# Third leaf and sums of the last gate/up pair on VectorE, another step order, and other first buffers for the down projection

## The chip, the cores and the metric

The kernel runs on one core of a Trainium2 chip. A core has a matrix engine (TensorE, "PE" in the profile, with its weight loads apart as "PEld"), an elementwise engine (VectorE, "DVE"), an engine for functions and copies (ScalarE, "ACT"), a general engine (GpSimd, "POOL"), and one that issues transfers (SyncE, "SP"). Matrix products land in eight PSUM banks and are read from there by VectorE or ScalarE. GpSimd's transfers can add what they bring to what lies at the target ("accumulating"). The metric is the device time of the whole program in microseconds, the median of three runs.

## What is computed

A block of a hybrid network on 1024 positions with a width of 1024: an mLSTM mixer and a sparse attention, their outputs merged, then a gated feed-forward part of width 2816. The change touches only the feed-forward part:

```python
h = h + mixed @ w_out[l]
f = rms_norm(h, g_norm_ffn[l])
h = h + (jax.nn.silu(f @ w_gate[l]) * (f @ w_up[l])) @ w_down[l]
...
return rms_norm(h, g_final)
```

## The kernel before

Everything is float32. A product is made of three matmuls (`chain3`): both operands are split into a high and a low part; high times high, high times low and low times high are added in PSUM. ScalarE copies the high part, VectorE subtracts it for the low part (`operand`, `op`).

**Gate and up.** The 2816 columns of w_gate and w_up are worked in 11 pairs of 128 columns, `s` = 0 to 10, each for gate (`G`, `w` = 0) and up (`U`, `w` = 1). A pair's product with the normed rows is done by a scheme with seven products in place of eight, numbered `q`; three of them (2, 4 and 3, the "leaves") are done by the same scheme once more, across gate and up. `whole` (L2578) does a product of the first level: q 6, 7, 1 and 5, in the step texts `g6`, `u7` and so on. `two` (L2616) does the leaves 2 and 4 (`d` for the pair before, `D` for the same pair), `third` (L2635) leaf 3 (`t` and `T`). `begin` loads the raw weights' first halves, `rest` the second ones. The raw weights lie in four buffers of 512 KB; `RB[s, w, 0]` holds the first half of the rows, `RB[s, w, 1]` the second; `RH` is the right part of the first.

The sums of raw weights are made in place. Some are made by VectorE (`combine`), others by accumulating transfers of GpSimd that fetch the addend from HBM again (`gather`). Behind product 7, leaf 3 needs the first half's left part to which the second half is added: two such transfers for each of gate and up. A third kind adds one result to another inside SBUF (`moved`). Gated results go to HBM, to `d_gu`, two rows for each pair.

**The order.** A step text (L2696) is gone through for the pairs 2 to 10; it gives each step a rank. A planner (`Plan`) then places the steps: each engine has a clock, each step a cost written out by hand and the steps that it depends on, and the step that can start first, or with the lower rank among those, is next on its engine. The engines then run their queues strictly in that order. `V5`, `V2` and `V1` are the costs of VectorE's operations; `lat` is the time to a transfer's landing that the planner assumes.

**The down projection** adds over 22 rows of `d_gu` in two groups of pairs (five and six), again with seven products in place of eight, `q` in the order 1, 5, 6, 3, 7, 2, 4 in the first group. `RSL` and `SLOTS` say which buffer takes which operand: numbers below 16 are `sl`, 16 to 27 `q`, 28 to 30 `ra`, from 36 on `lateU`. The late buffers lie where the low parts of the normed rows (`UTL`) lie, so they are free when the last product of gate and up has read those. The results of the first group are copied from PSUM into `acc`, and an accumulating transfer adds `d_h`, the sum so far, to each.

Of the kernel before, what the change touches and what calls it, by code (L numbers as in the profile page):

```python
# [8 lines left out]
F32 = mybir.dt.float32  # L9
F32R = mybir.dt.float32r  # L10
AF = mybir.ActivationFunctionType
ALU = mybir.AluOpType
# [171 lines left out]
def body(ctx, tc, a, out, stop=None, dbg=None):  # L184
# [46 lines left out]
    class Stream:  # L231
# [13 lines left out]
        def dma(self, upto):  # L245
            while self.nd <= min(upto, len(self.jobs) - 1):
                src, (n, m), *_ = self.jobs[self.nd]
                t = self.pool.tile([P, T], F32, name=f"raw{self.nd}", tag="raw", bufs=self.bufs)
                v = t[:, 0:n * m].rearrange("p (n m) -> p n m", n=n)
                col = 0  # L250
                for s in (src if isinstance(src, list) else [src]):
                    w = s.shape[-1]
                    nc.sync.dma_start(v[:, :, col:col + w], s)
                    col += w
                self.raw[self.nd] = v
                self.nd += 1
# [104 lines left out]
    with ExitStack() as sa:  # L361
# [60 lines left out]
        V = (("DVE", 700.0),)  # L422
# [1700 lines left out]
    def slot_ap(n, dt):  # L2123
        if n > 35:
            if not late:
                late.append(utp.tile([P, 8, 2, 512], F32R, name="lateU", tag="UTL", bufs=1))
            return cast32(late[0][:, n - 36]) if dt == F32 else late[0][:, n - 36]
        if n < 16:
            if n not in held or held[n].dtype != dt:
                held[n] = q2p.tile([P, 2, 512], dt, name=f"sl{n}_{len(held)}", tag=f"sl{n}", bufs=1)  # L2130
            return held[n]
        if n < 28:
            z = (n - 16) % 2
            return q1_tile((n - 16) // 2, dt)[:, 2 * z:2 * z + 2, :]
        if n < 31:
            return RAW[n - 28]
        return (WHI, WLO)[(n - 31) // 2][(n - 31) % 2]
# [194 lines left out]
    def rows4(b):  # L2332
        return b.ap.rearrange("p a (k c) -> p (a k) c", k=2)
# [18 lines left out]
    def col(s, w, z, h):  # L2352
        return lambda: rows4(RB[s, w, z])[:, :, h]
# [17 lines left out]
    def moved(b, x):  # L2371
        pl.step((("Pool", 850.0),), lambda e: nc.gpsimd.dma_start(b.ap, x.ap, accum_op=ALU.add), [x], [b], lat=5000.0)
# [7 lines left out]
    def combine(dst, x, y, alu, reads, writes):  # L2380
        ew(V5, dst, x, y, alu, reads, writes)
# [179 lines left out]
    def begin(s):  # L2561
        p = ST[s] = Pair()
        p.A, p.C = ([pl.buf(), pl.buf()] for _ in range(2))
        p.x, p.b = {2: pl.buf(), 4: pl.buf(), 3: pl.buf()}, {2: pl.buf(), 4: pl.buf(), 3: pl.buf()}
        p.out, p.own = {}, {}
        for w in range(2):
            load_raw(s, w, 0, w)
        for w in range(2):
            gather(RH[s, w], raw_src(s, w, 1, HI), col(s, w, 0, HI))
# [8 lines left out]
    def whole(s, q, w):  # L2578
        p, r0, rh, r1 = ST[s], RB[s, w, 0], RH[s, w], RB.get((s, w, 1))
        left = col(s, w, 0, LO)  # L2580
        if q == 6:
            combine(left, left, col(s, w, 0, HI), ALU.add, [rh], [r0])
        elif q == 7:
            combine(left, left, col(s, w, 1, HI), ALU.subtract, [r1], [r0])
            if w == U:
                gather(r1, raw_src(s, U, 1, k=1), row(s, U, 1, 0))
        level1(s, w, q)
        if q == 7:
            gather(r0, raw_src(s, w, 1, HI), left)
            gather(r0, raw_src(s, w, 1, LO), left)  # L2590
        acc_ = p.C if q == 5 else p.A
        product(s, w, q, acc_[w], q in (1, 5), q in (7, 5))
        t = p.out[q, w] = copied(acc_[w], place_of(s, q, w))
        if q == 5:
            moved(p.out[6, w], t)
            ew(V5, lambda: t.ap, lambda: t.ap, lambda: p.out[7, w].ap, ALU.add, [p.out[7, w]], [t])
            if w == 1:
                gated(s, 1, 1, p.out[5, G], p.out[5, U])
# [35 lines left out]

    def third(s, n):  # L2635
        p = ST[s]
        g, u = RB[s, G, 0], RB[s, U, 0]
        quarter = lambda r, k: (lambda: rows4(r)[:, 2 * k:2 * k + 2, LO])
        wa, wb, wc, wd = quarter(g, 0), quarter(u, 0), quarter(g, 1), quarter(u, 1)
        if n in PACKS:  # L2640
            b = slot_buf(RING4[nop[0] % 4], F32R)
            nop[0] += 1
            if n == 6:
                ew(V1, wb, wb, wd, ALU.add, [], [u])
                ew(V1, wa, wb, wa, ALU.subtract, [u], [g])
            elif n == 7:
                ew(V1, wc, wc, wa, ALU.subtract, [], [g])
                ew(V1, wa, wd, wa, ALU.subtract, [u], [g])
            for m, k in enumerate(PACKS[n]):
                form = lambda hl, m=m: b.ap[:, hl, 256 * m:256 * m + 256].rearrange("p (k c) -> p k c", k=2)  # L2650
                x, r = {1: (wa, g), 2: (wc, g), 6: (wa, g), 5: (wb, u), 7: (wa, g), 3: (wc, g), 4: (wd, u)}[k]
                act(400.0, lambda form=form: form(0), x, AF.Copy, [r], [b])
                ew(V1, lambda form=form: form(1), x, lambda form=form: cast32(form(0)), ALU.subtract, [r, b], [b])
                p.own[3, k] = b, m
        chains(s, p, 3, n)
        gathers(p, 3, n, p.out[6, G], p.out[6, U])
        if n == 4:
            gated(s, 0, 1, p.out[6, G], p.out[6, U])

    def run(s, text):  # L2660
        for t in text.split():
            kind, what = t[0], t[1:]
            if kind in "gu":
                whole(s, int(what), "gu".index(kind))
            elif kind == "d" and s - 1 >= 2:
                two(s - 1, int(what))
            elif kind == "D":
                two(s, int(what))
            elif kind == "t" and s - 1 >= 2:
                third(s - 1, int(what))  # L2670
            elif kind == "T":
                third(s, int(what))
            elif t == "begin" and s + 1 < NS:
                begin(s + 1)
            elif t == "rest":
                rest(s)

    flat(0)
    lates = []
    pl.boost = -60  # L2680
# [12 lines left out]
    last()  # L2693
    pl.boost = 0
    for s in range(2, NS):
        run(s, "g1 d3 u1 d4 rest g6 u6 t1 t2 g7 t6 t5 t7 t3 u7 t4 begin g5 D2 u5 D1 D6 D5 D7")  # L2696
    run(NS - 1, "D3 T1 T6 T2 T5 T7 D4 T3 T4")

# [2 lines left out]
    HEAD7, HEAD4, SUMMED = 3, 1, (0,)  # L2703
    OPS = (20, 21, 22, 23, 10, 13, 12, 15, 31, 33, 32, 34)
    OPL = list(OPS + (6, 7, 9, 3, 4, 8))
    RSL = (0, 24, 26, 28, 11, 1, 25, 27, 29, 14, 16, 18, 30, 36, 38, 17, 19, 2, 37, 5, 40, 41, 42, 43)
    LATE = 80
    V, SUM = V5, V5
    allf = list(fsb.values())
    gLb = slot_buf(39)  # L2710

    def load2(n, src, reads=()):

        bs = pieces(n)
        dma(lambda: slot_ap(n, F32), lambda: src.rearrange("p (a c) -> p a c", a=2), reads, bs, kb=512)
        return bs

    def op(src, n=None):
# [293 lines left out]
```

## Time and profile before

| | |
|---|---|
| median of three timed runs | 1534.38 us (1533.55 to 1534.68) |
| the profiled execution | 1532.0 us |
| its span | 1530.2 us |
| TensorE busy | 1509.6 us, 99% of the span |
| VectorE, ScalarE, GpSimd busy | 77%, 57%, 18% |
| HBM read and written | 169.95 and 62.48 MB |

A page gives each engine's busy time, groups of instructions by line, and the chain of waits that ended last. Rows of the timeline have a start and a duration in us, the engine, the line, what is written and read by the program's names, and in brackets the idle time of the engine before it and what ended it. A table of stretches has for each the busy time of PE, PEld, DVE, ACT and POOL with the number of instructions, then TensorE's granted clock, the DMA engines' busy share and GB/s. A busy TensorE may still run at half the clock; the column says so.

### The profile page before, as it was taken

To read this page: it belongs to the slowest core of one execution; us is meant where nothing else is said; L and a number is where in the kernel's file an instruction comes from. 1 tells how busy PE (TensorE), PEld (TensorE's weight loads), DVE (VectorE), ACT (ScalarE), POOL (GpSimd) and SP (SyncE) were. 2 spreads that over 40 slices of the span, in tenths; PEclk is the share of its full clock that TensorE was granted. 3 is DMA by queue.
4 is the path that set the end of the run, shared out by engine and by line. 5 is a ranking of instruction groups with operands and counts; after the bars stand their busy time and mean duration, and the time that the engine had idled before them with its cause. 6 is when DMAs were issued, how large, how long until landed. Compare 5 with 4: busy or idle time off the path is not lost.

```text
span 1530.2 us, 23966 instructions
## 1 busy us (share of the span) xinstructions
PE 1509.6 (99%) x8274; PEld 1304.4 (85%) x8274; DVE 1181.0 (77%) x2540; ACT 874.8 (57%) x1940; POOL 282.1 (18%) x399
## 2 busy tenths in 40 slices
PE   9999999999999999999999999999999998999997
PEld 8978888888988888888888888888888887888886
DVE  7877878456988798956665596778777776898996
ACT  8535444576988798865453464445445544465443
POOL 7500003333100111011020012222222222110000
PEclk9999999999999999999999999999999999999999
DMA  7458657859232622128466245477777779857002
GB/s 250 155 137 247 203 184 242 245 201 260 70 90 66 162 70 87 43 62 301 133 210 189 83 125 125 75 145 145 152 145 151 153 145 253 263 124 234 1 1 111
DMA packets 201924, 230.93 MB, mean 151 GB/s; under 512 B 11978, under 2 KB 156487, under 8 KB 201546
## 3 DMA queue, kind: packets, MB, share of 16 engines
q1 hardware_dynamic: 152090, 188.22, 38.2%
q0 software_dynamic: 49424, 40.85, 17.2%
q8 instruction: 65, 1.06, 0.3%
q14 instruction: 57, 0.47, 0.1%
q10 hardware_dynamic: 288, 0.33, 0.1%
HBM read 169.95 MB, written 62.48 MB: 152 GB/s over the span
## 4 chain that ended last, share of the span: by engine, by line
PE 93%; DMA 3%; DVE 2%; ACT 1%; issue 0%; SPq 0%; POOL 0%; DVEq 0%; POOLq 0%; ACTq 0%
PE PS L2330 38%; PE PSA L309 6%; PE PSA L311 6%; PE PSA L310 6%; PE T L1634 4%; PE d L309 3%; PE d L310 3%; PE d L311 3%; PE obank L1665 2%; PE obank L1667 2%; PE PS L309 2%; PE PS L311 2%; PE br L310 2%; PE br L309 2%; PE PS L310 2%; PE br L311 2%
## 5 line engine op out<-in xcount | busy, mean ns | idle before, releaser
L2091 DVE TENSOR_TENSOR sl<-PS,sl 128x256 f32<-128x256 f32 (+1 forms) x202 | 100.5, 510 | 71.6 <-PE PS L2330 58.8
L2330 PE MATMUL PS<-sl,sl 128*128 128x512 f32 (+1 forms) x513 | 118.5, 385 | 0.0
L2330 PEld LDWEIGHTS PS<-sl,sl 128*128 128x128 f32 x513 | 95.3, 188 | 19.4 <-DVE acc L2091 0.2
L2094 ACT ACTIVATE sl<-PS 128x512 f32<-128x512 f32 x90 | 53.7, 598 | 94.2 <-PE PS L2330 73.6
L1654 DVE TENSOR_TENSOR TL<-T,TH 128x512 fp32r<-128x512 f32 (+1 forms) x151 | 90.6, 617 | 19.4 <-ACT TH L1645 17.8
L2330 PE MATMUL PS<-q,wh 128*128 128x512 f32 x420 | 101.2, 391 | 0.0
L2330 PE MATMUL PS<-UTH,wl 128*128 128x256 f32 (+1 forms) x392 | 97.7, 323 | 1.2 <-ACT wl L2094 1.0
L2330 PEld LDWEIGHTS PS<-q,wh 128*128 128x128 f32 x420 | 77.3, 188 | 15.0
L1645 ACT ACTIVATE TH<-T 128x512 fp32r<-128x512 f32 (+1 forms) x151 | 79.3, 539 | 18.6 <-PE T L1634 16.8
L2330 PE MATMUL PS<-q,wl 128*128 128x512 f32 x348 | 84.2, 391 | 0.0
L2330 PE MATMUL PS<-UTH,wh 128*128 128x256 f32 (+1 forms) x344 | 82.4, 315 | 0.0
L1665 PE MATMUL obank<-TH,VHL 128*128 128x256 f32 x263 | 75.6, 310 | 0.0
L2330 PEld LDWEIGHTS PS<-UTH,wl 128*128 128x128 f32 x392 | 68.8, 193 | 7.6 <-ACT wl L2094 1.2
L2330 PEld LDWEIGHTS PS<-q,wl 128*128 128x128 f32 x348 | 63.8, 188 | 12.3
L2091 DVE TENSOR_TENSOR sl<-sl,sl 128x512 f32<-128x512 f32 (+2 forms) x87 | 57.2, 662 | 21.9 <-DMA d_h<-sl 10.1
L309 PE MATMUL d<-UTH,whi 128*128 128x512 f32 x176 | 71.4, 406 | 0.1
L311 PE MATMUL d<-UTH,wlo 128*128 128x512 f32 x176 | 69.1, 393 | 0.0
L310 PE MATMUL d<-UTL,whi 128*128 128x512 f32 x176 | 69.0, 392 | 0.0
L1667 PE MATMUL obank<-TL,VHL 128*128 128x256 f32 x264 | 68.2, 282 | 0.0
L2094 ACT ACTIVATE sl<-sl 128x512 f32<-128x512 f32 (+1 forms) x73 | 44.4, 625 | 40.4 <-DVE sl L2091 26.6
L309 PE MATMUL PSA<-UTH,wOwhi 128*128 128x512 f32 (+1 forms) x172 | 67.1, 390 | 0.0
L311 PE MATMUL PSA<-UTH,wOwlo 128*128 128x512 f32 (+1 forms) x180 | 66.9, 372 | 0.0
(1392 smaller groups left out, 4654.4 us busy)
## 6 DMA issues: line engine op xcount, KB each, us to landing
d_gu<-sl SPq DMA_DIRECT2D x44, 256.0 KB, 2.8
rA<-in_w_in SPq DMA_DIRECT2D x18, 512.0 KB, 4.9
q<-d_mg SPq DMA_DIRECT2D x32, 256.0 KB, 3.4
ra<-in_w_gate SPq DMA_DIRECT2D x16, 512.0 KB, 5.7
d_rep<-d_row SPq DMA_DIRECT2D x8, 960.0 KB, 6.9
sl<-in_w_up POOLq DMA_DIRECT2D x29, 256.0 KB, 5.3
ra<-in_w_up SPq DMA_DIRECT2D x12, 512.0 KB
raw<-in_w_in SPq DMA_DIRECT2D x10, 512.0 KB, 4.7
```

The source lines that it names most:

```text
L309: nc.tensor.matmul(ps, ah, bh, start=first, stop=False)
L310: nc.tensor.matmul(ps, ah, bl, start=False, stop=False)
L311: nc.tensor.matmul(ps, al, bh, start=False, stop=last)
L1634: nc.tensor.transpose(pt[:, z, P * r:P * r + P], e, ident)
L1645: nc.scalar.activation(hl[0][:, 0:m], pt[:, 0:m], AF.Copy)
L1654: nc.vector.tensor_tensor(hl[1][:, 0:m], pt[:, 0:m], cast32(hl[0])[:, 0:m], ALU.subtract)
L1665: nc.tensor.matmul(po, vv, th[:, z, :], start=(st[1] == 0), stop=False)
L1667: nc.tensor.matmul(po, vv, tl[:, z, :], start=False, stop=(st[1] == st[2]))
L2091: return pl.step(alts, lambda e: ENG[e].tensor_tensor(out_(), x(), y(), alu), reads, writes, **kw)
L2094: return pl.step((("ACT", cost),), lambda e: nc.scalar.activation(out_(), x(), fn, scale=scale), reads, writes, **kw)
L2330: nc.tensor.matmul(ps, x, y, start=first and n == 0, stop=last and n == 2, skip_group_check=True)
```

## The change

The last pair (s = 10) is treated apart. In `whole`, ahead of the difference for product 7, VectorE writes the left part plus the second half's left part into a buffer of its own, `p.last[w]`, from which `third` then takes leaf 3's weights; the four transfers that made the same sum in place are gone for this pair. Up's sum of two row blocks, for which a transfer fetched one again, is made by VectorE from what lies there. The two results that `moved` added are added by VectorE. Ahead of the last pair the planner's costs of VectorE's operations are set to 625, 350 and 350 (`quick`). The last pair has a step text of its own, in which leaf 3 of pair 9 comes early, and its own leaves behind. In the down projection the operands of the first group take other buffers (`RSL`), VectorE's cost is 690 again, and the planner assumes that a load lands after 5000 and not 2000 as long as the results of no product have been copied.

```diff
@@ -2581,18 +2581,27 @@
         elif q == 7:
+            if s == NS - 1:
+                d = p.last[w] = piece(w)
+                combine(lambda: four(d.ap), left, col(s, w, 1, LO), ALU.add, [r0, r1], [d])
             combine(left, left, col(s, w, 1, HI), ALU.subtract, [r1], [r0])
-            if w == U:
+            if w == U and s == NS - 1:
+                combine(row(s, U, 1, 0), row(s, U, 1, 0), row(s, U, 1, 1), ALU.add, [], [r1])
+            elif w == U:
                 gather(r1, raw_src(s, U, 1, k=1), row(s, U, 1, 0))
         level1(s, w, q)
-        if q == 7:
+        if q == 7 and s < NS - 1:
             gather(r0, raw_src(s, w, 1, HI), left)
             gather(r0, raw_src(s, w, 1, LO), left)
...
         if q == 5:
-            moved(p.out[6, w], t)
+            if s < NS - 1:
+                moved(p.out[6, w], t)
+            else:
+                v = p.out[6, w]
+                ew(V5, lambda: v.ap, lambda: v.ap, lambda: t.ap, ALU.add, [t], [v])
@@ -2634,8 +2643,11 @@
-        g, u = RB[s, G, 0], RB[s, U, 0]
-        quarter = lambda r, k: (lambda: rows4(r)[:, 2 * k:2 * k + 2, LO])
+        g, u = (p.last.get(w, RB[s, w, 0]) for w in (G, U))
+        if p.last:
+            quarter = lambda r, k: (lambda: four(r.ap)[:, 2 * k:2 * k + 2])
+        else:
+            quarter = lambda r, k: (lambda: rows4(r)[:, 2 * k:2 * k + 2, LO])
@@ -2675,6 +2687,10 @@
+    def quick():
+        nonlocal V5, V2, V1
+        V5, V2, V1 = (("DVE", 625.0),), (("DVE", 350.0),), (("DVE", 350.0),)
@@ -2693,8 +2709,10 @@
     for s in range(2, NS):
-        run(s, "g1 d3 u1 d4 rest g6 u6 t1 t2 g7 t6 t5 t7 t3 u7 t4 begin g5 D2 u5 D1 D6 D5 D7")
-    run(NS - 1, "D3 T1 T6 T2 T5 T7 D4 T3 T4")
+        if s == NS - 1:
+            quick()
+        run(s, "t1 g1 u1 t6 t2 t5 t7 d3 d4 g6 t3 t4 u6 rest g7 g5 u7 D1 D6 D2 u5 D5 D7 D3 T1 T6 T2 T5 D4 T7 T3 T4" if s == NS - 1 else "g1 d3 u1 d4 rest g6 u6 t1 t2 g7 t6 t5 t7 t3 u7 t4 begin g5 D2 u5 D1 D6 D5 D7")
+    run(NS - 1, " ")
@@ -2703,16 +2721,16 @@
-    RSL = (0, 24, 26, 28, 11, 1, 25, 27, 29, 14, 16, 18, 30, 36, 38, 17, 19, 2, 37, 5, 40, 41, 42, 43)
+    RSL = (24, 26, 30, 28, 11, 25, 27, 16, 29, 14, 17, 18, 0, 36, 38, 1, 19, 2, 37, 5, 40, 41, 42, 43)
-    V, SUM = V5, V5
+    V = SUM = V5 = (("DVE", 690.0),)
...
-        dma(lambda: slot_ap(n, F32), lambda: src.rearrange("p (a c) -> p a c", a=2), reads, bs, kb=512)
+        dma(lambda: slot_ap(n, F32), lambda: src.rearrange("p (a c) -> p a c", a=2), reads, bs, kb=512, lat=5000.0 if not acct else 2000.0)
```

Three places in the engines' queues. First GpSimd, from the end of pair 9 to the start of the copies into `acc`. Before (the rows of w_gate and w_up, and the two from `sl` to `sl` behind them, belong to the last pair; those of w_down to the down projection's first sums):

```order
L2369 DMA ra_8650<-in_w_gate 128x4x128
L2369 DMA ra_8649<-in_w_up 128x2x256
L2734 DMA q_4_6_12593<-in_w_down 128x512
L2369 DMA sl_1_8686<-in_w_up 128x4x128
L2369 DMA ra_8650<-in_w_gate 128x4x128
L2734 DMA q_5_6_12606<-in_w_down 128x512
L2734 DMA sl_16_9345<-in_w_down 128x512
L2369 DMA sl_1_8686<-in_w_up 128x4x128
L2372 DMA sl_16_9354<-sl_16_9435 128x512 x2
L2734 DMA sl_16_12841<-in_w_down 128x512
L2734 DMA ra_8649<-in_w_down 128x512
```

The same place of the changed kernel:

```order
L2752 DMA q_4_6_12654<-in_w_down 128x512
L2752 DMA q_5_6_12672<-in_w_down 128x512
L2752 DMA q_0_6_12798<-in_w_down 128x512
L2752 DMA sl_16_12831<-in_w_down 128x512
L2752 DMA ra_8649<-in_w_down 128x512
```

The seven transfers of the last pair are gone; the five sums of w_down are there in both.

Second TensorE, at the end of gate and up. The rows of `UTH` and `UTL` are the last pair's last product, those with two `sl`, or with `wl` and `wh`, or `q`, are products of the down projection. Before:

```order
L2330 MATMUL PS_8646<-UTH,wh_8652 128x256
L2330 MATMUL PS_8646<-UTL,wh_8652 128x256
L2330 MATMUL PS_8646<-UTH,wh_8652 128x256 x2
L2330 MATMUL PS_8646<-UTL,wh_8652 128x256
L2330 MATMUL PS_8646<-UTH,wh_8652 128x256
L2330 MATMUL PS_8642<-sl_16_9650,sl_16_9475 128x512 x3
L2330 MATMUL PS_8641<-sl_16_9650,sl_16_9475 128x512 x3
L2330 MATMUL PS_8645<-sl_16_9650,sl_16_9475 128x512 x3
L2330 MATMUL PS_8643<-sl_16_9650,sl_16_9475 128x512 x3
L2330 MATMUL PS_8642<-sl_16_9748,sl_16_9594 128x512 x3
```

The changed kernel:

```order
L2330 MATMUL PS_8647<-sl_16_9748,sl_16_9594 128x512 x3
L2330 MATMUL PS_8642<-sl_16_9748,sl_16_9594 128x512 x3
L2330 MATMUL PS_8641<-sl_16_9748,sl_16_9594 128x512 x3
L2330 MATMUL PS_8640<-sl_16_9748,sl_16_9594 128x512 x3
L2330 MATMUL PS_8646<-UTH,wh_8652 128x256
L2330 MATMUL PS_8646<-UTL,wh_8652 128x256
L2330 MATMUL PS_8646<-UTH,wh_8652 128x256 x2
L2330 MATMUL PS_8646<-UTL,wh_8652 128x256
L2330 MATMUL PS_8646<-UTH,wh_8652 128x256
L2330 MATMUL PS_8647<-wl_8653,wh_8651 128x512 x3
```

The products with `sl_16_9650` and `sl_16_9748`, twelve matmuls each, stood behind the last product and now stand ahead of it. The product of the third pair in the third step (q = 6) reads buffers of the same names again, `sl_16_9748` and `sl_16_9594`; from the last product of gate and up to there stand 40 rows of three matmuls before, and 32 in the changed kernel.

Third SP, the loads into the late buffers and the load behind them. Before:

```order
L2105 DMA lateU<-d_gu_132 128x1024
L2105 DMA lateU<-in_w_down 128x1024
L2105 DMA lateU<-d_gu_134 128x1024
L2105 DMA lateU<-d_gu_136 128x1024
L2105 DMA lateU<-d_gu_138 128x1024
L2105 DMA lateU<-d_gu_140 128x1024
L2105 DMA d_gu_145<-sl_16_9354 128x512
L2105 DMA lateU<-d_gu_142 128x1024
L2105 DMA lateU<-in_g_final 128x1024
L2105 DMA sl_16_9354<-in_w_down 128x1024
```

The changed kernel:

```order
L2105 DMA lateU<-d_gu_132 128x1024
L2105 DMA lateU<-in_w_down 128x1024
L2105 DMA lateU<-d_gu_134 128x1024
L2105 DMA d_gu_145<-sl_16_9354 128x512
L2105 DMA lateU<-d_gu_136 128x1024
L2105 DMA lateU<-d_gu_138 128x1024
L2105 DMA lateU<-d_gu_140 128x1024
L2105 DMA lateU<-d_gu_142 128x1024
L2105 DMA lateU<-in_g_final 128x1024
L2105 DMA sl_16_9354<-in_w_down 128x1024
```

The write of a gated result from `sl_16_9354`, for which the load into the same buffer waits, moved from the seventh to the fourth place.

More of the change, by code (lines that the diff above doesn't have):

```diff
@@ L2564, in begin @@
         p.x, p.b = {2: pl.buf(), 4: pl.buf(), 3: pl.buf()}, {2: pl.buf(), 4: pl.buf(), 3: pl.buf()}
-        p.out, p.own = {}, {}
+        p.out, p.own, p.last = {}, {}, {}
         for w in range(2):
```

## The prediction

> **What bounds the kernel now.** First the head of the page, then the table of stretches, which says where TensorE (PE) is not busy.
>
> ```profile
> span 1530.2 us, 23966 instructions
> PE 1509.6 (99%) x8274; PEld 1304.4 (85%) x8274; DVE 1181.0 (77%) x2540; ACT 874.8 (57%) x1940; POOL 282.1 (18%) x399
> 900.00:1250.00 350.00, 350.00 (x1970) 307.19 (x1969) 269.74 (x502) 170.96 (x311) 93.63 (x78) 1.00 0.68 138
> 1250.00:1312.00 62.00, 53.70 (x308) 47.46 (x308) 43.98 (x89) 28.19 (x55) 12.78 (x13) 0.94 0.85 220
> 1312.00:1520.00 208.00, 208.00 (x945) 173.22 (x944) 184.97 (x320) 106.29 (x200) 14.08 (x16) 1.00 0.39 118
> ```
>
> TensorE sets the end nearly everywhere. From 900 us on it is idle in one place only, 1250 to 1312 us, for 62.00 − 53.70 = 8.3 us, and there its granted clock is 0.94 and not 1.00. That place is the last gate/up pair with the first loads of the down projection. The changed kernel issues the same matmuls, so only this loss can be won, and only new idle time can be lost. TensorE's rows in the order of time give its pieces (in brackets the idle time before each):
>
> ```profile
> 1255.15 1.70 PE L2330 MATMUL PS<-sl,wl 128*128 128x256 f32 x12 [1.10 <-DVE sl L2091]
> 1282.96 0.39 PE L2330 MATMUL PS<-UTH,wl 128*128 128x256 f32 x1 [1.03 <-ACT wl L2094]
> 1283.68 0.51 PE L2330 MATMUL PS<-UTH,wl 128*128 128x256 f32 x2 [0.22 <-DVE wl L2091]
> 1291.00 0.95 PE L2330 MATMUL PS<-sl,wh 128*128 128x256 f32 x6 [0.90 <-DVE sl L2091]
> 1296.08 0.74 PE L2330 MATMUL PS<-sl,wh 128*128 128x256 f32 x4 [3.05 <-DVE wh L2091]
> 1298.83 1.65 PE L2330 MATMUL PS<-sl,wh 128*128 128x256 f32 x6 [2.00 <-DVE sl L2091]
> ```
>
> The sum is 8.30 us. VectorE and ScalarE are named, but they waited themselves; their own rows, and the chain of waits, say for what:
>
> ```profile
> 1253.95 0.69 DVE L2091 TENSOR_TENSOR sl<-sl,sl 128x512 f32<-128x512 f32 x1 [2.08 <-DMA sl<-sl]
> 1281.76 0.63 ACT L2094 ACTIVATE q<-sl 128x512 fp32r<-128x512 f32 x1 [3.56 <-DMA sl<-in_w_down]
> 1295.00 0.43 DVE L2091 TENSOR_TENSOR sl<-sl 128x256 f32<-128x256 f32 x1 [2.59 <-DMA sl<-in_w_up]
> 1297.62 0.69 DVE L2091 TENSOR_TENSOR sl<-sl,sl 128x512 f32<-128x512 f32 x1 [1.59 <-DMA sl<-sl]
> ...
> 1275.63 10.29 DMA sl<-in_w_up
> 1287.77 9.83 DMA sl<-sl
> 1298.83 46.21 PE PS L2330 x226
> ```
>
> Accumulating transfers of GpSimd, 10.29 and 9.83 us long, carry the chain to TensorE's row at 1298.83; the 3.05 us hang on another of them, for which VectorE waits at 1295.00. The 1.03 at 1282.96 is ScalarE's queue: a down-projection copy of w_down stands ahead of a gate/up copy and waits for its load. The idle time has a second price, seen when the stretch is cut into pieces of 6.8 us:
>
> ```profile
> 1284.40:1291.20 6.80, 5.90 (x39) 5.23 (x38) 6.10 (x11) 4.41 (x9) 2.21 (x2) 1.00 1.14 198
> 1291.20:1298.10 6.90, 2.57 (x18) 2.09 (x17) 2.52 (x6) 2.18 (x5) 0.86 (x1) 1.00 1.09 296
> 1298.10:1304.90 6.80, 6.07 (x26) 5.98 (x27) 5.13 (x11) 2.39 (x5) 0.00 (x0) 0.50 0.72 258
> 1516.60:1523.40 6.80, 4.60 (x36) 4.28 (x35) 4.84 (x21) 2.70 (x8) 0.00 (x0) 1.00 0.21 78
> 1523.40:1530.20 6.80, 0.00 (x0) 0.00 (x0) 1.71 (x5) 1.09 (x2) 0.00 (x0) 0.50 0.42 157
> ```
>
> A piece with 4.3 idle us is followed by one at clock 0.50; so is, at the program's end, a piece with 2.2 idle us. A piece with 0.9 is not. The half clock made 6.07 busy us do the work of 3.04. So the loss to be won is 8.30 + 3.04 = 11.3 us.
>
> **The change part by part.** *Removed:* seven GpSimd transfers of the last pair, two into each first half of gate and up, one into up's second half, two of one result into another. They hold both ends of the chain above. *Added:* five VectorE operations of 128x512 with both operands in SBUF: two sums kept for the third leaf, one sum of up's rows, two sums of results. The 1297.62 row has the price of one, 0.69 us: 3.45 us in all. VectorE is busy 43.98 of the 62.00 us, so 18 us of idle time cover them; without cover each would cost TensorE up to 0.69.
>
> *Moved:* the third leaf of pair 9 stands earlier. The last pair's second-half loads (two of 512 KB on SP) are issued in the other order; their consumers stand behind other operations that TensorE still has work ahead of. I cost this at nothing, with bounds 0 and 2 us. *The planner's cost for loads* (5000 for 2000) puts ScalarE's copies of w_down behind the gate/up copies, so the 1.03 and the 0.22 go too. SP's writes of gated results and GpSimd's sums of w_down (five, as before) remain; with seven transfers fewer beside them they land no later.
>
> *What is late next* inside the pair: where a PSUM bank must be emptied by VectorE directly ahead of the next product, TensorE waits for part of an operation of 0.42 to 0.69. The new order has two tight places of this kind, near 1254 and 1293 us. The nearest row is the 1.10; below it stands nothing at all. I take 0.3 + 0.5 = 0.8, with bounds 0 and 2.1 (three operations of 0.69).
>
> *What is late next* behind the pair is the large term. The region of the late buffers becomes free with the pair's last product, and from there SP sends a burst of loads; the last of them, w_down into `sl_16_9354`, is an operand of the sums for the third pair's third product:
>
> ```profile
> 1316.82 0.32 SPq L2105 DMA_DIRECT2D lateU<-d_gu  x1
> 1329.50 0.33 SPq L2105 DMA_DIRECT2D sl<-in_w_down  x1
> ...
> 1338.01 0.69 DVE L2091 TENSOR_TENSOR q<-q,sl 128x512 f32<-128x512 f32 x1 [2.50 <-DMA sl<-in_w_down]
> 1338.61 1.14 ACT L2094 ACTIVATE sl<-q 128x512 fp32r<-128x512 f32 x2
> ...
> 1316.74 5.63 PE L2330 MATMUL PS<-sl,sl 128*128 128x512 f32 x24
> 1341.25 4.92 PE L2330 MATMUL PS<-sl,sl 128*128 128x512 f32 x21
> ```
>
> From the burst's start to the landing pass 1338.0 − 1316.8 = 21.2 us, and VectorE already waits 2.50 us for it. TensorE doesn't: it has 120 matmuls of 512 columns between the pair's last product and the one that needs this operand (40 rows of three in its order). From 1316.74 to 1341.25 it does 108, so 0.227 us each, 27.2 us for 120. The subtraction takes 0.69 more, and a copy about as long (1.14 for two), together some 1.4 with the hand-over: ready at 22.6, needed at 27.2, 4.6 us to spare. In the changed order two products of the down projection, 24 matmuls, stand ahead of the pair's last product. Behind it remain 96 (32 rows of three): needed at 96 × 0.227 = 21.8 us after the burst's start. The 4.6 to spare become −0.8, if the load takes as long as before.
>
> It will take a little longer. The load itself is issued earlier, since the write of a gated result that must land before it now stands fourth in the burst, not seventh; but the loads in front of it are the same. Beside it run GpSimd's accumulating transfers into the result tile, in two groups of four:
>
> ```profile
> 1323.98 3.52 POOL L2734 DMA_DIRECT2D acc<-d_h  x4 [12.73 <-ACT acc L2951]
> 1340.52 3.52 POOL L2734 DMA_DIRECT2D acc<-d_h  x4 [13.02 <-ACT acc L2951]
> ...
> 1317.00:1324.00 7.00, 7.00 (x32) 5.80 (x31) 7.00 (x14) 2.73 (x5) 0.02 (x1) 1.00 0.99 365
> 1329.00:1340.00 11.00, 11.00 (x50) 9.12 (x49) 7.39 (x13) 5.29 (x10) 0.00 (x0) 1.00 0.78 199
> ```
>
> In the changed order both groups come some 5.4 us (24 matmuls) sooner against the burst: the first at 2 to 4 us instead of 7.2, the second by 23.7 − 5.4 = 18.3 us, inside the 21 us. At 365 GB/s a transfer of 256 KB takes about 0.7 us, at 199 GB/s 1.3. One of 1.3 more in the time before the landing gives 22.5; none, and an emptier queue ahead of the burst (less 3 × 0.7), 19; the whole second group, 4 × 1.3, 26.4. I take 22.5, near the 21.2 of the row. Ready at 22.5 + 1.4 = 23.9, needed at 21.8: TensorE waits 2.1, and 0.7 more for VectorE's low part after the first matmul. **2.8 us**, with bounds 0 (19 us) and 6.7 (26.4).
>
> Then the half clock: 2.8 idle us within some 3 us stand above the 2.2 that halved the clock at the end, and above the 0.9 that didn't, unless the border of two pieces splits them. I take one half-clock piece: between the 3.04 of the row and 6.8 / 2 = 3.4, 3.3 us; bounds 0 and 6.8.
> The Trainium skill ("TensorE: Matmul & The Clock Gate", section "Why this matters for your kernels") asks for no idle gaps of TensorE over about 3 us, and lets one idle window bring the half clock back. By that rule a wait of 2.8 us costs no clock, and the sum would be the second case below; the row of 2.2 idle us at the end speaks against it.
>
> **Sum.** Won 11.3; lost 0.8 + 2.8 + 3.3 = 6.9; net 4.4 us. The profiled execution took 1532.0 us (span 1530.2 and 1.8 around it), the median of the timed runs is 1534.4. The difference of 2.4 is carried over: 1534.4 − 4.4 = **1530.0**.
>
> **The rivals.**
> 1. *No half clock after the new wait.* For it: the longest wait is shorter than the 3.05 of before, and the border may split it. 11.3 − 3.6 = 7.7 won: 1526.7.
> 2. *The load lands in time.* Seven transfers fewer have left the queues empty ahead of the burst. Against it: the spare time shrinks by 5.4 us. 11.3 − 0.8 = 10.5 won: 1523.9.
> 3. *The waits only change their names.* The 3.05 and 2.00 were VectorE's queue, and it gets five operations more and none fewer; if the gate/up pair keeps waiting for its raw loads and the burst is late as well, the loss stays about 11: 1534.4, no change.
> 4. *Slower.* The load of the third sums is served behind both groups of accumulating transfers: 26.4 + 1.4 − 21.8 + 0.7 = 6.7 us of waiting, which spoils two pieces, 6.8 us of clock. 0.8 + 6.7 + 6.8 = 14.3 lost against 11.3 won: 1537.4. It decides from a landing about 26 us after the burst's start; for it speak the 199 GB/s while such transfers run.
>
> **How the numbers follow.** A measurement of this kernel can tell about 0.2%, 3.1 us, from no change. Chances: forecast 0.50, no half clock 0.22, load in time 0.10, no change 0.10, slower 0.08. The forecast's own spread (0.8 and 2.8 are uncertain by 1 to 2 us) leaves a fifth of it above 1531.3. Faster 0.39 + 0.22 + 0.10 = 0.71; same 0.11 + 0.10 = 0.21; slower 0.08. The range from 1525.0 to 1534.5 takes in the forecast, the first rival and no change with their spread, and leaves out the second and the last, 0.18.
>
> **What would show it.** In the changed profile, between 1250 and 1312 us no wait of TensorE over about 1 us, no 128x512 DMA wait ahead of VectorE there, and GpSimd's rows of w_gate and w_up ending with pair 9. Some 22 us after the first load into the late buffers, a wait of TensorE for ScalarE and VectorE, behind a VectorE row that waits for w_down, then a piece at clock 0.50. Wrong it would be if TensorE waits over 2 us inside the gate/up pair, if the load lands under 20 us after the burst's start, or if TensorE waits elsewhere in the down projection, whose buffers and order have changed throughout.

## The result, and the profile after

| | before | after |
|---|---|---|
| median | 1534.53 us (1532.75 to 1537.28, 6 runs) | 1527.38 us (1524.84 to 1528.18, 6 runs) |
| profiled execution | 1532.0 us | 1524.84 us |
| its span | 1530.2 us | 1523.0 us |

The ratio is 0.9949, with a 95% interval from 0.9937 to 0.9962: 7.15 us faster, where 4.4 us were forecast. The measured median lies nearer to the first rival's 1526.7 us than to the forecast's 1530.0.

The head of the page after, with the same two lines as before:

```profile
span 1523.0 us, 23961 instructions
PE 1508.3 (99%) x8274; PEld 1301.5 (85%) x8274; DVE 1185.0 (78%) x2545; ACT 874.6 (57%) x1940; POOL 273.1 (18%) x392
```

TensorE's work is the same; VectorE has five instructions more and GpSimd seven fewer. The table of stretches after (columns as before):

```profile
900.00:1250.00 350.00, 349.38 (x1962) 305.94 (x1961) 269.10 (x500) 170.99 (x313) 92.11 (x77) 1.00 0.68 137
1250.00:1312.00 62.00, 61.54 (x379) 55.24 (x379) 57.97 (x116) 33.12 (x65) 5.96 (x7) 1.00 0.75 213
```

From 1250 to 1312 us TensorE's idle time fell from 8.30 to 0.46 us, and the clock is 1.00. VectorE rose from 44 to 58 busy us of 62: it does the added work, and work that used to come later. TensorE's rows after that have idle time ahead of them in the changed part:

```profile
1294.71 0.36 PE L2330 MATMUL PS<-UTH,wl 128*128 128x256 f32 x1 [0.43 <-DVE sl L2091]
1336.25 0.50 PE L2330 MATMUL PS<-sl,sl 128*128 128x512 f32 x1 [0.33 <-ACT sl L2094]
1337.39 2.83 PE L2330 MATMUL PS<-sl,sl 128*128 128x512 f32 x11 [0.64 <-DVE sl L2091]
```

The first is one of the two tight places, and the other two stand where the prediction put its new wait, with 0.97 us in place of 2.8. The burst's start, the load and its landing, from the rows of SP's queue and of VectorE:

```profile
1313.72 0.32 SPq L2105 DMA_DIRECT2D lateU<-d_gu  x1
...
1321.80 0.33 SPq L2105 DMA_DIRECT2D sl<-in_w_down  x1
1334.84 0.69 DVE L2091 TENSOR_TENSOR q<-q,sl 128x512 f32<-128x512 f32 x1 [4.01 <-DMA sl<-in_w_down]
```

The load landed 1334.84 − 1313.72 = 21.1 us after the burst's start; 22.5 were forecast. No half clock followed in this execution: in this it is the first rival's case.

The part from 1250 to 1345 us won more than the program did: 10.3 us by the table of the experiments below, against 7.2 us between the two profiled executions. Up to its 7000th matmul TensorE has the same order in every kernel here. It starts that matmul at 1248.0 us in before's trace, at 1251.4 in the changed kernel's, and at 1249.1 to 1251.3 in the twelve traces of the experiments. So before's trace is the quickest up to there, and the 3.4 us that the changed kernel's comes later hide a part of what it wins behind. What makes this difference stays open.

### The profile page after: what moved, and what is told of

The parts are those of the page before. It is cut to its first block, busy times and chain, and to the rows that moved or that the text cites. A ratio compares the mean times of both kernels' runs of the same rounds, so it can differ in the third digit from the quotient of the medians.

```text
span 1523.0 us, 23961 instructions
## 1 busy us (share of the span) xinstructions
PE 1508.3 (99%) x8274; PEld 1301.5 (85%) x8274; DVE 1185.0 (78%) x2545; ACT 874.6 (57%) x1940; POOL 273.1 (18%) x392
## 4 chain that ended last, share of the span: by engine, by line
PE 90%; DMA 5%; DVE 3%; ACT 1%; issue 1%; POOL 0%; DVEq 0%; POOLq 0%; ACTq 0%
PE PS L2330 36%; PE PSA L309 6%; PE PSA L311 6%; PE PSA L310 6%; PE T L1634 4%; PE d L309 3%; PE d L311 3%; PE d L310 3%; PE obank L1665 2%; PE obank L1667 2%; PE PS L310 2%; PE PS L311 2%; PE br L311 2%; PE br L310 2%; PE PS L309 2%; PE br L309 2%
## 5 line engine op out<-in xcount | busy, mean ns | idle before, releaser
L1654 DVE TENSOR_TENSOR TL<-T,TH 128x512 fp32r<-128x512 f32 (+1 forms) x151 | 90.7, 618 | 19.4 <-ACT TH L1645 17.7
L2330 PE MATMUL PS<-q,wh 128*128 128x512 f32 x408 | 98.1, 390 | 0.0
L2330 PE MATMUL PS<-UTH,wl 128*128 128x256 f32 (+1 forms) x380 | 94.5, 324 | 0.4 <-DVE sl L2091 0.4
L2330 PEld LDWEIGHTS PS<-UTH,wh 128*128 128x128 f32 x356 | 60.8, 190 | 4.4
```

The lines of the kernel that those rows point to most:

```text
L1654: nc.vector.tensor_tensor(hl[1][:, 0:m], pt[:, 0:m], cast32(hl[0])[:, 0:m], ALU.subtract)
L2330: nc.tensor.matmul(ps, x, y, start=first and n == 0, stop=last and n == 2, skip_group_check=True)
```

## The experiments

Three things changed together: who makes the sums (the engine swap), the step order, and the first buffers with the planner's cost of loads. The first four runs take them apart, the next four leave one out or repeat the whole, and the last four move one load or return one kind of transfer. In the table, "loss" is TensorE's idle time from 1250 to 1345 us in the profiled execution (waits over 0.15 us) plus half of the time at clock 0.50 in that part (idle time inside a stretch at half clock is counted in both, so the longest are a little too high).

The planner places the steps anew for each edit, so TensorE's order can move with it. It is that of before in run 3 and that of the changed kernel in runs 5, 7 and 9; in all other runs it is one of its own. What those cost or win is the edit together with the planner's answer to it.

| run | ratio to before, 95% interval | median against before, us | idle + half clock, us | loss, us |
|---|---|---|---|---|
| before | 1 | | 8.30 + 6.83 | 11.7 |
| after | 0.9949 [0.9937, 0.9962] | −7.2 | 1.40 + 0 | 1.4 |
| 1 swap alone | 0.9997 [0.9989, 1.0006] | −0.4 | 8.09 + 6.83 | 11.5 |
| 2 order alone | 1.0009 [1.0000, 1.0018] | +1.8 | 7.41 + 10.24 | 12.5 |
| 3 buffers alone | 1.0039 [1.0027, 1.0051] | +5.3 | 11.55 + 13.65 | 18.4 |
| 4 all but the swap | 1.0042 [1.0030, 1.0054] | +6.0 | 11.53 + 13.65 | 18.4 |
| 5 after again | 0.9957 [0.9943, 0.9971] | −6.6 | 3.88 + 6.83 | 7.3 |
| 6 all but the buffers | 1.0032 [1.0020, 1.0044] | +5.9 | 10.90 + 13.65 | 17.7 |
| 7 all but the load cost | 0.9959 [0.9945, 0.9973] | −6.3 | 2.92 + 0 | 2.9 |
| 8 all but the order | 0.9981 [0.9970, 0.9991] | −2.3 | 4.86 + 3.41 | 6.6 |
| 9 one load earlier | 0.9932 [0.9918, 0.9945] | −11.4 | 0.42 + 0 | 0.4 |
| 10 leaf sums back | 1.0011 [1.0002, 1.0020] | +1.5 | 8.82 + 13.65 | 15.6 |
| 11 result sums back | 0.9995 [0.9985, 1.0004] | −1.3 | 6.39 + 3.41 | 8.1 |
| 12 row sum back | 0.9975 [0.9965, 0.9985] | −4.8 | 5.17 + 3.41 | 6.9 |

The loss of one execution, less before's 11.7, follows the median of the runs to about 3 us. So TensorE's waits at this one place, and the clock that they cost, are in the main what moves the time in all these kernels.

### 1. The engine swap alone

```diff
+        if q == 7 and s == NS - 1:
+            combine(left, left, col(s, w, 1, HI), ALU.add, [r1], [r0])
+            combine(left, left, col(s, w, 1, LO), ALU.add, [r1], [r0])
+            if w == U:
+                combine(row(s, U, 1, 0), row(s, U, 1, 0), row(s, U, 1, 1), ALU.add, [], [r1])
...
+                v = p.out[6, w]
+                ew(V5, lambda: v.ap, lambda: v.ap, lambda: t.ap, ALU.add, [t], [v])
```

> The kernel before with the seven GpSimd transfers of the last pair made by VectorE instead, and nothing else: old step order, old buffers, old cost of loads. Since the old order keeps the buffer of p.last in use, the third leaf's weights are made in place here, with two VectorE operations for gate and two for up behind product 7, so seven operations replace seven transfers. Theory of the prediction (the transfers' 10 us landings hold TensorE up): the waits of 3.05 and 2.00 us and the half clock of 3.04 us go, those of 1.10, 1.03 and 0.22 stay, 0.90 may: 7 to 9 us faster than before, no 128x512 DMA wait ahead of VectorE in 1285 to 1300 us. Rival A (the new step order wins it, by giving the same transfers more time): the chain only changes to VectorE's queue, within 2 us of before, a wait of over 2 us still near 1290 to 1300 us. Rival B (VectorE's queue is the limit there): seven operations of 0.69 us more, 2 to 5 us slower than before.

No difference that can be told from none, which is rival A's time, and the chain moved to VectorE's queue, as rival A has it. (Its reason, that the order alone wins, falls with run 2.) The stretch around the largest wait in this kernel, then rows of ScalarE, VectorE and TensorE there:

```profile
1287.50:1298.80 11.30, 5.99 (x36) 5.24 (x35) 10.95 (x20) 3.91 (x7) 0.86 (x1) 0.79 0.79 253
```

```profile
1285.20 0.63 ACT L2094 ACTIVATE q<-sl 128x512 fp32r<-128x512 f32 x1 [4.33 <-DMA sl<-d_gu]
1286.91 0.69 DVE L2091 TENSOR_TENSOR wl<-ra,wl 128x512 fp32r<-128x512 f32 x1 [3.81 <-ACT wl L2094]
...
1292.31 2.74 DVE L2091 TENSOR_TENSOR sl<-sl,sl 128x512 f32<-128x512 f32 x4
1295.15 0.69 DVE L2427 SCALAR_TENSOR_TENSOR sl<-sl 128x512 f32<-128x512 f32 x1
1295.76 0.75 DVE L2091 TENSOR_TENSOR sl<-PS,sl 128x256 f32<-128x256 f32 x2
...
1296.33 3.34 PE L2330 MATMUL PS<-sl,wh 128*128 128x256 f32 x12 [4.36 <-DVE sl L2091]
```

The waits for GpSimd's transfers are gone, and VectorE works 10.95 of 11.30 us. TensorE waits for the emptying of a bank at 1295.76, which stands behind five operations on other results: four sums, two of them among the added, and a gated product. But a load has its part in it: just ahead of this stretch ScalarE's queue stood 4.33 us for a load of `d_gu`, a down-projection operand in its old buffer, and VectorE 3.81 us for ScalarE, so its work came late. In run 8, with the new buffers and cost of loads and the same order, this wait is gone and 2.11 of TensorE's 4.36 us are left. The changed kernel has VectorE just as full in the same stretch, and TensorE hardly waits:

```profile
1287.50:1298.80 11.30, 10.87 (x70) 9.76 (x69) 10.76 (x22) 6.71 (x14) 0.86 (x1) 1.00 0.78 249
```

So what decides there is not how busy VectorE is but what TensorE waits for in its queue.

### 2, 3 and 4. The order alone, the buffers alone, and both without the swap

The second kernel has the new step text and `quick`, the third the lines below; the fourth is the change without the three places that replace transfers.

```diff
-    RSL = (0, 24, 26, 28, 11, 1, 25, 27, 29, 14, 16, 18, 30, 36, 38, 17, 19, 2, 37, 5, 40, 41, 42, 43)
+    RSL = (24, 26, 30, 28, 11, 25, 27, 16, 29, 14, 17, 18, 0, 36, 38, 1, 19, 2, 37, 5, 40, 41, 42, 43)
...
-reads, bs, kb=512)
+reads, bs, kb=512, lat=5000.0 if not acct else 2000.0)
```

> The kernel before with the new step text for the last pair and the new VectorE costs alone: the transfers stay with GpSimd, buffers and cost of loads stay old. Theory of the prediction: the transfers still take about 10 us each to land and stand ahead of VectorE, so at least half of the 8.30 us of waiting stays in 1250 to 1315 us, only at other places, and a half clock with it: 0 to 4 us faster than before. Rival A (the order wins it): waits below 2.5 us in sum inside the pair and 6 to 9 us faster than before, what the whole change gives or near it.

> The kernel before with the new first buffers of the down projection and the later landing of loads in the plan alone: old order, old transfers. Theory of the prediction: the 1.03 and 0.22 us at 1283 us (ScalarE's copies of w_down ahead of gate/up copies) go, the large waits for the transfers stay: 0 to 2 us faster. Rival C (buffers and load cost carry the gain): over 4 us faster. The other side: loads of the first sums go into buffers that come free later in the old order, so TensorE waits behind the pair and it is 1 to 4 us slower.

> The whole change without the engine swap: new order, new buffers, new cost of loads, but all seven transfers of the last pair stay with GpSimd. Theory of the prediction: the gain falls to less than half, 0 to 3 us faster than before, with VectorE waiting at 1285 to 1310 us for transfers from sl to sl or from in_w_up. Rival A (order): as fast as the changed kernel within 1.5 us, so 5.5 to 8.5 us faster than before.

None is faster than before, and two are slower by more than was expected: three expectations of the theory missed on the same side. (For the buffers alone the expectation also named another side, a wait behind the pair and 1 to 4 us lost; its place is right, its size too small.) The rows of VectorE that wait for transfers, and those of TensorE behind them, with the order alone:

```profile
1282.55 0.69 DVE L2091 TENSOR_TENSOR ra<-ra,ra 128x512 f32<-128x512 f32 x1 [4.24 <-DMA ra<-in_w_up]
1293.99 0.69 DVE L2091 TENSOR_TENSOR sl<-sl,sl 128x512 f32<-128x512 f32 x1 [4.28 <-DMA sl<-sl]
1304.39 0.42 DVE L2091 TENSOR_TENSOR sl<-sl 128x256 f32<-128x256 f32 x1 [5.76 <-DMA sl<-in_w_up]
...
1295.20 0.98 PE L2330 MATMUL PS<-sl,wh 128*128 128x256 f32 x6 [3.57 <-DVE sl L2091]
1306.66 0.58 PE L2330 MATMUL PS<-UTH,wh 128*128 128x256 f32 x1 [2.65 <-ACT wh L2094]
```

All three kinds of transfer, up's row sum, a result's sum and the leaf's sum, now have a wait of their own. With the buffers alone, in the old order, TensorE waits at the old place and once more behind the pair, where ScalarE's copy waits for a load into `ra` that is issued only at 1313.93:

```profile
1296.03 1.22 PE L2330 MATMUL PS<-sl,wh 128*128 128x256 f32 x4 [5.62 <-DVE wh L2091]
1313.93 0.38 SPq L2105 DMA_DIRECT2D ra<-d_gu  x1
1319.71 0.63 ACT L2094 ACTIVATE sl<-ra 128x512 fp32r<-128x512 f32 x1 [2.42 <-DMA ra<-d_gu]
1320.39 7.11 PE L2330 MATMUL PS<-sl,sl 128*128 128x512 f32 x24 [4.46 <-ACT sl L2094]
```

With both and no swap, the first two large waits again stand behind VectorE's waits for transfers from `sl` to `sl`:

```profile
1288.31 0.69 DVE L2091 TENSOR_TENSOR sl<-sl,sl 128x512 f32<-128x512 f32 x1 [4.88 <-DMA sl<-sl]
1306.17 0.69 DVE L2091 TENSOR_TENSOR sl<-sl,sl 128x512 f32<-128x512 f32 x1 [3.83 <-DMA sl<-sl]
...
1289.59 0.80 PE L2330 MATMUL PS<-sl,wh 128*128 128x256 f32 x2 [4.35 <-DVE sl L2091]
1307.97 0.58 PE L2330 MATMUL PS<-UTH,wl 128*128 128x256 f32 x1 [4.53 <-DVE sl L2091]
1321.97 7.68 PE L2330 MATMUL PS<-sl,sl 128*128 128x512 f32 x24 [2.16 <-ACT sl L2094]
```

### 5 to 8. The change again, and less one part

The fifth kernel is the changed one. The sixth has the old `RSL`, the seventh no `lat=5000.0`, the eighth is the swap of run 1 with the lines of run 3.

> The changed kernel once more, unaltered, beside the three below on one chip: 6 to 9 us faster than before (it was 7.15). If waits of TensorE under 1 us don't bring the half clock, its trace again shows clock 1.00 from the program's first 15 us to TensorE's last matmul. If the difference between the profiled gain of the stretch (about 10 us) and the median's 7 is half clock in some executions, this trace or the spread of the times shows it.

> The changed kernel with the old list of first buffers; engine swap, new order and cost of loads stay. In the old list the first load goes into slot 0, which the third leaf's weights p.last occupy until the leaf is split at the pair's end. Theory (the engine swap frees TensorE only if the first loads do not wait for a buffer that the swap keeps busy): ScalarE and TensorE wait for that load and those behind it on SP near 1295 to 1312 us, 4 to 10 us of waiting with a half clock: about the time of before or up to 5 us slower. Rival (the buffers are only a detail, swap and order together carry the gain): within 2 us of the changed kernel.

> The changed kernel with the landing of loads planned at 2000 and not 5000; all else stays. The prediction put the going of the 1.03 and 0.22 us to this cost: if that is right, ScalarE's copies of w_down stand ahead of gate/up copies again and TensorE waits 1 to 2 us more in 1275 to 1300 us: 1 to 2 us slower than the changed kernel. Rival: the loads land before these copies are reached anyway, since the new buffers let them start earlier; then within 1 us, and the later wait of 0.97 us at 1336 us may change by up to 1 us either way, since the copies for the third sums move too.

> Engine swap (weights of the third leaf in place, seven VectorE operations) and new buffers and cost of loads, with the old step text. The swap alone left VectorE without a pause from 1287 to 1299 us and TensorE waiting 4.36 us for its queue, and ScalarE 4.33 us for a load of d_gu. Theory (VectorE's queue needs the new order to take the added operations): the ScalarE wait goes with the new buffers, the 4.36 us stay within 2 us, half clock with them: 0 to 4 us faster than before. Rival (the order is not needed once transfers are gone and buffers are free): as fast as the changed kernel within 2 us.

The repeat gives nearly the same gain, but its profiled execution took 1529.39 us, the longest of its six. The burst, the load and the waits (SP, VectorE, TensorE), then the stretches from the wait on:

```profile
1313.26 0.32 SPq L2105 DMA_DIRECT2D lateU<-d_gu  x1
...
1322.75 0.33 SPq L2105 DMA_DIRECT2D sl<-in_w_down  x1
1336.87 0.69 DVE L2091 TENSOR_TENSOR q<-q,sl 128x512 f32<-128x512 f32 x1 [6.90 <-DMA sl<-in_w_down]
1338.28 0.80 PE L2330 MATMUL PS<-sl,sl 128*128 128x512 f32 x1 [3.11 <-ACT sl L2094]
1339.42 0.79 PE L2330 MATMUL PS<-sl,sl 128*128 128x512 f32 x1 [0.35 <-DVE sl L2091]
```

```profile
1331.10:1337.90 6.80, 4.06 (x18) 3.02 (x17) 1.03 (x2) 0.31 (x1) 1.49 (x2) 1.00 1.11 241
1338.00:1344.70 6.70, 6.08 (x13) 4.42 (x14) 6.70 (x12) 5.64 (x11) 0.00 (x0) 0.50 0.08 14
```

Here the load landed 23.6 us after the burst's start, TensorE waited 3.46 us, and the half clock came. This is the prediction's forecast, seen in one execution; the first trace, with 21.1 us, is the first rival. The load was issued 9.5 us after the burst's start here and 8.1 there. Why the same program does now one and now the other stays open.

Without the new buffers (run 6) TensorE waits 6.20 us for the first products of the down projection. SP's row of the load into slot 0, and the rows that it ends:

```profile
1305.13 0.32 SPq L2105 DMA_DIRECT2D sl<-d_gu  x1
1312.76 0.69 DVE L2091 TENSOR_TENSOR sl<-sl,q 128x512 f32<-128x512 f32 x1 [1.81 <-DMA sl<-d_gu]
1313.44 6.72 PE L2330 MATMUL PS<-q 128*128 128x512 f32 x16 [6.20 <-ACT q L2094]
```

Slot 0 holds the third leaf's weights of gate and up, so this load, the old list's first, is issued only at 1305.13. (ScalarE's queue had stood 3.56 us for a load of w_down as well, until 1311.63.) The swap moved the sum into a buffer, and the list of buffers had to make room for it. The theory named the place; the loss is somewhat above its range, and the rival falls.

The load cost (run 7) makes no difference in the median, as its rival said. The prediction's 1.03 and 0.22 us do not come back near 1283 us; other waits appear from 1308 to 1316, 0.54 and 0.78 us for ScalarE and 0.31 us for VectorE behind it.

Without the new order (run 8) the gain shrinks to 2.3 us. TensorE's largest wait and the stretches around it:

```profile
1291.77 0.47 PE L2330 MATMUL PS<-sl,wh 128*128 128x256 f32 x2 [2.11 <-DVE sl L2091]
```

```profile
1290.10:1293.50 3.40, 1.36 (x9) 1.19 (x10) 3.30 (x7) 0.00 (x0) 0.86 (x1) 1.00 0.98 363
1293.60:1296.90 3.30, 3.30 (x17) 3.30 (x17) 1.94 (x5) 1.85 (x4) 0.00 (x0) 0.50 0.72 185
1297.00:1300.40 3.40, 2.25 (x19) 2.05 (x18) 3.40 (x9) 1.53 (x3) 0.00 (x0) 1.00 0.14 19
```

It is again VectorE's queue, full from end to end (3.30 of 3.40 us and 3.40 of 3.40). The 4.36 us of run 1 became 2.11, a little more of a change than the theory allowed; the time, 4.3 us behind run 5, is the theory's and not the rival's. The middle row is the price on the clock, 3.41 us at 0.50.

### 9. The late load ahead of those that nobody waits for

```diff
-        dma(...)
+        st = dma(..., behind=ahead[0] if ahead and n >= 40 else None)
+        if n == 2 and not ahead:
+            ahead.append(st)
...
-[gLb], kb=512)
+[gLb], kb=512, behind=ahead[0])
```

> The changed kernel with one load moved in SP's queue: the w_down load for the third sums, which lands last before the new wait, now stands right behind the write of the gated result that it must follow, five places earlier, ahead of the second group's loads into the late buffers and of g_final. TensorE's and GpSimd's orders are untouched; the copy and the subtraction that use the load move up a few places on ScalarE and VectorE. Theory (the new wait is that load's place behind five others of 512 KB): it lands 5 to 8 us sooner, at most 17 us after the burst's start (21.1 and 23.6 in the two traces of the changed kernel), TensorE's wait near 1336 us and the half clock behind it go: 1 to 4 us faster than the changed kernel, 8 to 11 faster than before, and a narrower spread. Rival (GpSimd's eight accumulating transfers set the landing, wherever the load stands): landing still past 20 us, time within 1 us of the changed kernel.

SP's and VectorE's rows, and TensorE's only wait over 0.15 us from 1250 us on:

```profile
1312.15 0.32 SPq L2105 DMA_DIRECT2D lateU<-d_gu  x1
...
1320.13 0.33 SPq L2105 DMA_DIRECT2D sl<-in_w_down  x1
1327.33 0.69 DVE L2091 TENSOR_TENSOR q<-q,sl 128x512 f32<-128x512 f32 x1 [0.92 <-DMA sl<-in_w_down]
1293.13 0.35 PE L2330 MATMUL PS<-UTH,wl 128*128 128x256 f32 x1 [0.42 <-DVE sl L2091]
```

The load lands 15.2 us after the burst's start. It is issued no earlier (8.0 us after, since it still follows the write), but lands 7.2 us after its issue and not 13 to 14. The median is 1522.38 us (1521.40 to 1522.84): this version is 11.4 us faster than before and, on the ratios, 0.0017 to 0.0025 or 2.6 to 3.8 us faster than the changed kernel's two sets (the intervals overlap by 0.0008 and 0.0002, so the size is rough), and its spread is 1.4 us where the changed kernel's two sets had 3.3 and 5.7. GpSimd's accumulating transfers, which the rival blamed, were not touched, and the rival's landing past 20 us did not come. But the load now lands ahead of their second group, which starts at 1329.86 us; how much that group adds to a landing of 21 to 24 us this run does not tell.

### 10, 11 and 12. One kind of transfer returned to GpSimd

Ten has the four transfers of `whole` back (`gather` into `r0`, no `p.last`), eleven the two of `moved`, twelve the one `gather` of up's row sum; all else is the changed kernel.

> The changed kernel with the four transfers for the third leaf's weights returned to GpSimd (in place, as before); up's row sum and the two sums of results stay with VectorE. Theory of the prediction (these hold the pair's last chain): VectorE waits near 1300 to 1312 us for transfers from in_w_up or in_w_gate, TensorE for 4 to 7 us in sum, with a half clock: 4 to 9 us slower than the changed kernel. Rival (two of the seven carry it all, these four are hidden): within 1.5 us of the changed kernel.

> The changed kernel with the two transfers that add one result to another returned to GpSimd; the other five stay with VectorE. In before, TensorE's 2.00 us and VectorE's 1.59 us at 1297 us hung on one of them. Theory: in the new order the results' leaves stand later, so the transfers have more time; 0 to 3 us slower than the changed kernel, waits from sl to sl ahead of VectorE near 1295 us. The other side: two VectorE operations fewer where VectorE is busy 58 of 62 us, up to 1 us faster.

> The changed kernel with one transfer returned to GpSimd: up's sum of two row blocks, which up's fifth product and the leaves 2 and 4 read from. Theory: one transfer of some 5 to 10 us stands between product 7 of up and the leaves, which follow at once in the new order: VectorE or ScalarE waits for it near 1285 us, TensorE 2 to 4 us: 2 to 6 us slower than the changed kernel. Rival: the leaves that need it stand late enough; within 1 us.

Each return costs: against run 5, by the ratios, 0.0054 (8 us), 0.0038 (6 us) and 0.0018 (3 us). Together they would be 17 us where the whole gain is 7, so the parts don't add up. One reason can be that a wait at one of them takes the time in which the others could land; another is that each run has an order of its own. Run 12 came out as the theory expected, though its cost is hardly beyond the noise; run 11 cost about twice the 3 us at most of its expectation. The result sums (run 11) and the row sum (run 12), each with VectorE's row and TensorE's behind it:

```profile
1303.92 0.69 DVE L2091 TENSOR_TENSOR sl<-sl,sl 128x512 f32<-128x512 f32 x1 [3.64 <-DMA sl<-sl]
1305.73 0.58 PE L2330 MATMUL PS<-UTH,wl 128*128 128x256 f32 x1 [4.23 <-DVE sl L2091]
```

```profile
1287.39 0.69 DVE L2091 TENSOR_TENSOR ra<-ra,ra 128x512 f32<-128x512 f32 x1 [2.44 <-DMA ra<-in_w_up]
1289.07 1.18 PE L2330 MATMUL PS<-q,wh 128*128 128x512 f32 x3 [3.36 <-DVE wh L2091]
```

With the leaf sums back (run 10) the time is as expected, but not the place: VectorE waits there for no transfer from in_w_up or in_w_gate. The largest wait, 6.00 us, stands behind the pair, for ScalarE's copies of operands of the down projection. SP's row of one load of these operands, first in the changed kernel and then in run 10:

```profile
1278.64 0.36 SPq L2105 DMA_DIRECT2D ra<-d_gu  x1
1309.21 0.32 SPq L2105 DMA_DIRECT2D ra<-d_gu  x1
```

Made in place, the leaf's weights keep gate's raw buffer to the pair's end, and the new list gives that buffer to this load, as in run 3. The 24 matmuls of two `sl` that stand ahead of the pair's last product in the changed kernel stand behind it here. VectorE waits for this load until 1316.04 us, and ScalarE for a load of w_down until 1316.96; how the 6.00 us divide between the two stays open. So run 10 takes back a part of the buffers and of the order too, and its 8 us are no price of the four transfers alone.

## Why the prediction was right, and where it was not

- *The loss to be won, 11.3 us.* Right in size: the kernel that has almost none of it left (run 9, 0.4 us) is 11.4 us faster.
- *"They hold both ends of the chain": the removal of the transfers as the whole cause.* Half right. Without it nothing is won (run 4), and to return any one kind costs time (10 to 12, with the planner's new orders in it). But the removal alone wins nothing either (run 1). The prediction costed the order at nothing, within 2 us, and gave the buffers no price; given the other parts, they are worth some 4 us (run 8 against run 5) and some 12 us (run 6 against run 5). The forecast's time did not suffer, because the three came together; so its number is right there by luck, and not by its account.
- *Five VectorE operations hidden in 18 us of its idle time.* They are hidden in the changed kernel, but idle time is no cover by itself: only 4 us of it are left there, and in run 1 TensorE waited for a bank behind a full VectorE queue with two of the added sums in it. The third rival, that the waits only change their names, is what the swap alone does: VectorE's queue, and ScalarE's behind a load, in place of GpSimd's transfers.
- *The planner's cost takes the 1.03 and 0.22 away.* Not so: they stay away without it (run 7).
- *The tight places, 0.8 us.* One of the two was seen, with 0.42 to 0.43 us.
- *The new wait, 2.8 us, and one half-clock piece, 3.3 us.* Place and mechanism right, and shown by run 9 but for the share of GpSimd's second group. The step that failed is the size: both were counted in full, as one case, where the executions show two. The traces give 0.97 + 0 and 3.46 + 3.04 (half of 6.08 busy us at clock 0.50), and at the median the removal of both is worth 2.6 to 3.8 us, not 6.1. The forecast was 2.6 us too slow, which is about what these two terms had too much; it is not shown that the differences ahead of the pair, up to 3.4 us between traces, have no part in it. The load's landing, estimated at 22.5 us, came at 21.1 and 23.6: a difference of 2.5 us lies across the point where the half clock starts.
- *The 2.4 us between profiled execution and median* were 2.5 in the changed kernel, but in run 5 the profiled execution lay 3.8 us above the median: this is no constant to carry over.

On the clock, the prediction took 0.9 idle us as harmless and 2.2 as enough. From 1060 us on to TensorE's end, no single wait up to 1.65 us is followed by a stretch at 0.50 in these traces, and each wait from 2.11 us on is followed by one or falls into one. (The one wait between, 2.00 us in before, ends in the stretch behind the 3.05.) Short ones can add up: in run 10 a piece at 0.50 begins at 1309.8, behind waits of 0.61 and 1.32 us. The Trainium skill ("TensorE: Matmul & The Clock Gate", section "Why this matters for your kernels") gives gaps over about 3 us; the wait of 2.11 us in run 8 differs, and the measurement decides.

## What to carry to other kernels

When a slow helper's work moves to a busy engine, the gain depends on what stands in that engine's queue ahead of the operation that the bound engine waits for, so the order has to change with the swap, and the buffers that the swap takes must not be those of the next stage's first loads. A burst of loads into newly freed buffers should be sorted by when each is needed: one load moved ahead of five that nobody waited for was worth some 3 us. Where a planner answers each edit with a new order, a run that takes one part out shows that part and the new order together, so the engines' queues have to be compared as well as the times. And a cost that sits on a threshold, here a landing that moves by 2.5 us from one execution to the next, is better priced as two cases than as one sum.

## What the runs showed of the hardware

The stretches at half clock inside the program were 3.41, 6.83, 10.24 or 13.65 us long, all multiples of 3.41, where the prediction had known only one of 6.8. The wait of 2.11 us cost 3.41 us at half clock, so, by an estimate of half of it, another 1.7 us: nearly as much as the wait itself.
